# Whole modulation units through GpSimd's queue inside a recurrence

## The chip, the cores and the metric

The kernel runs on one core of one Trainium2 chip. The metric is device time in microseconds (us) of one execution, as the median of several. Engines are named as in the profile: PE is TensorE (matrix products), PEld its weight loads, DVE is VectorE, ACT is ScalarE, POOL is GpSimd and SP is SyncE. SP, ACT and POOL can each issue DMA transfers from their own instruction queue; every engine executes its queue in order.

## The reference, cut to what matters

One inference step through two layers of width 2048, for 128 context tokens and 256 latent tokens. Layer 0 runs a bidirectional RWKV-7 recurrence next to a Fourier mixer, layer 1 is windowed attention. The change concerns the modulation: each layer needs twelve blocks of 512 columns of `silu(cond) @ mod_w + mod_b`, for two conditioning vectors.

```python
def _modulation(cond, w, b):
    m = (jax.nn.silu(cond) @ w + b)[..., None, :]
    return jnp.split(m, 3, axis=-1)
...
    for layer in range(DEPTH):
        i = layer // 2
        sh_p, sc_p, g_p = _modulation(c_ctx, mod_w[layer], mod_b[layer])
        sh_s, sc_s, g_s = _modulation(c, mod_w[layer], mod_b[layer])
        hp = _rmsnorm(xp, norm_pre[layer]) * (1.0 + sc_p) + sh_p
        hs = _rmsnorm(xs, norm_pre[layer]) * (1.0 + sc_s) + sh_s
```

## The kernel before

One 512-column block of the modulation has a weight matrix of 2048 x 512 floats, 4 MB, stored as four units of 1 MB. A unit (index `u`) is 128 partitions of 2048 floats: four row blocks of 512 columns. On PE a unit takes four float32 products, each into another quarter of the rows of one PSUM tile (`ps_mod`, line 322). After the fourth unit ACT copies the sums to SBUF (`mrow`, line 327), PE folds the quarters and turns them into columns (`ps_mt`, line 331), and DVE adds the bias (line 333).

Of the 24 blocks, 8 are done at the start (`mraw`, lines 598 on), 7 inside the recurrence of layer 0 (`FILL_MODS`, the lane `fill_lane`, the tiles `rawf`), 2 on PE and 7 by sums on DVE later (`PE_MODS`, `DVE_MODS`).

The recurrence works on eight pairs of heads. Its program is written by lanes (generators), which `weave` merges by a planner's costs: each `yield pe, dve, time` says what a step costs PE and DVE and how long it lasts, and the next step comes from the lane that can start first. The lanes are the projections (`proj_cm`, products `acc`, three per weight tile: lines 398 to 400), the elementwise part (`wkv_elem`), the scores, a triangular solve (`wkv_solve`, a long run of small DVE operations, then small products `ps_z`), the chain over time (`wkv_chain`) and the norm. The fill lane puts a modulation step between them, one in every `FILL_PACE` planned microseconds. What is written first goes into an engine's queue first, with priorities shifting it a little.

Projection weights come as tiles `raw` of 256 KB through SP's queue (line 234) into two buffers; ACT splits off a rounded part `whi` (line 258), DVE the remainder `wlo` (line 259). In the recurrence the fill lane's transfers stand in the same queue of SP (line 759): each is half a unit (256 of the 512 columns of each row block, 512 KB), into two buffers. POOL does nothing but fill small tiles: `p` (line 926) and `SV` (line 1106), once per pair of heads each.

Of the kernel before, what the change touches and what calls it, by code (L numbers as in the profile page):

```python
# [11 lines left out]
F32 = mybir.dt.float32  # L12
# [15 lines left out]


FILL_MODS = [(0, 8), (0, 9), (0, 10), (0, 11), (1, 0), (1, 4), (1, 1)]  # L30
FILL_PACE = 5
PE_MODS = [(1, 5), (1, 2)]
DVE_MODS = [(1, 6), (1, 3), (1, 7)], [(1, 8), (1, 9), (1, 10), (1, 11)]

# [169 lines left out]
class Stream:  # L204
# [13 lines left out]
    def load(self):  # L218
        k = self.k
        while self.next is not None:  # L220
            x = self.next
            if x[0] == "m" and x[2] and x[2] < 4:

                self.raws.append((x, self.raw))
                self.next = next(self.it, None)
                continue
            q, n, size = (x[0],) + ((k.RAWB, 512) if x[0] == "w" else (k.MODB, 2048))
            shared = len(x) == 3 and x[2] == 0
            if self.held[q] >= n or shared and self.held["m"]:
                return  # L230
            if shared:
                self.held["m"] = k.MODB
            raw = (k.rawp if q == "w" else k.mpool).tile([128, size], F32, name="raw", tag="raw" + q, bufs=n)
            k.nc.sync.dma_start(raw, x[1])
            if q == "m":
                self.raw = raw
            self.raws.append((x, raw))
            self.held[q] += 1
            self.next = next(self.it, None)
# [64 lines left out]
class K:  # L304
# [4 lines left out]
    def mod_unit(self, raw, layer, b, u, dst, c0=0):  # L309

        nc = self.nc
        key = layer, b, c0
        n = raw.shape[1] // 4
        if u == 0:
            self.macc[key] = self.pw.tile([128, 512], F32, name="ps_mod", tag="pw")
        acc = self.macc[key]
        for i in range(4):  # L320
            kt = 4 * u + i
            nc.tensor.matmul(acc[32 * i:32 * i + 32, :n], self.silu[:, 2 * kt:2 * kt + 32], raw[:, n * i:n * i + n],  # L322
                             start=(u == 0), stop=(u == 3), skip_group_check=True)
        if u < 3:
            return
        rows = self.mpool.tile([128, n], F32, name="mrow", tag="junk", bufs=1)
        nc.scalar.copy(rows, acc[:, :n])  # L327
        ps = self.pw.tile([128, 512], F32, name="ps_mt", tag="pw")
        m0, nm = c0 // 128, n // 128
        for m in range(nm):  # L330
            nc.tensor.matmul(ps[:, 2 * m:2 * m + 2], rows[:, 128 * m:128 * m + 128], self.sel, start=True, stop=True)
        m1 = 48 * layer + 4 * b + m0
        nc.vector.tensor_tensor(dst[:, m0:m0 + nm], ps[:, 0:2 * nm].rearrange("p (m c) -> p m c", c=2),
                                self.modb[:, m1:m1 + nm].unsqueeze(2).to_broadcast([128, nm, 2]), op=ALU.add)
        del self.macc[key]
# [308 lines left out]
    def layer0_mix(self):  # L644
        tc, nc, A = self.tc, self.nc, self.A
# [25 lines left out]
        kp = self.kp = self.open("kp", "right")  # L671
# [79 lines left out]
        def fill_lane():  # L751

            self.mpool = kp
            jobs = [(layer, b, self.mod_dst(layer, b), c0, u) for layer, b in FILL_MODS for c0 in (0, 256) for u in range(4)]

            def load(layer, b, dst, c0, u):
                raw = kp.tile([128, 4, 256], F32, name="rawf", tag="rawf", bufs=2)
                w = self.mod_w(layer, b, u).rearrange("p (k c) -> p k c", k=4)
                nc.sync.dma_start(raw, w[:, :, c0:c0 + 256])
                return raw.rearrange("p k c -> p (k c)")  # L760

            raws = [load(*x) for x in jobs[:2]]
            for n, (layer, b, dst, c0, u) in enumerate(jobs):
                yield 0.5, 0, FILL_PACE
                self.mod_unit(raws.pop(0), layer, b, u, dst, c0)
                if n + 2 < len(jobs):
                    raws.append(load(*jobs[n + 2]))

        self.weave(main_lane(), chain_lane(0), chain_lane(1), norm_lane(), elem_lane((0, 2, 3, 4, 5, 6, 7)), elem_lane((1,)), proj_lane(), fill_lane(),
                   lead=LEAD)  # L770
        self.close("kp")
# [121 lines left out]
    def wkv_elem(self, j, st):  # L893

        nc, kp = self.nc, self.kp
        TT, STT, ACT = nc.vector.tensor_tensor, nc.vector.scalar_tensor_tensor, nc.scalar.activation
        SD, uni, seg = self.SD, self.uni, self.seg
        r, k, v = st["r"], st["k"], st["v"]

        yield 0.8, 0, 2.3  # L900
        up = kp.tile([128, 2, 128], F32, name="up", tag="up", bufs=1)
        nc.scalar.dma_start(up, self.A["up"][j])
        if j == 1:

            w = kp.tile([128, self.WORK], F32, name="work0", tag="work", bufs=1)
            kk, sq = w[:, 0:T], w[:, T:2 * T]
            p = w[:, 768:1548].rearrange("p (v t) -> p v t", t=65)
            tha = w[:, 1548:2316].rearrange("p (v t) -> p v t", t=64)
            E = self.TI.rearrange("p u t -> p (u t)")[:, 0:780].rearrange("p (v t) -> p v t", t=65)
        else:  # L910
            kk = kp.tile([128, T], F32, name="kk", tag="kk", bufs=1)
            sq = kp.tile([128, T], F32, name="sq", tag="tmp", bufs=1)
            p = kp.tile([128, 12, 65], F32, name="p", tag="p", bufs=1)
# [71 lines left out]
        a, b = j % 2, 2 + j % 4  # L985
# [525 lines left out]
```

## Time and profile before

| | |
|---|---|
| median of 3 runs | 1658.42 us (1656.85 to 1660.56) |
| the profiled execution | 1664.2 us |
| its span, first to last instruction | 1662.4 us |
| PE busy | 1573.7 us, 95% of the span |
| DVE busy | 1126.3 us, 68% |
| ACT busy | 774.1 us, 47% |
| POOL busy | 3.7 us |

Half units are worked on from 135.7 to 528.2 us of the span. A float32 product appears in the trace as two records, so 56 half units of four products are 448 records. A busy PE is not PE at its peak: the ends of its records are modelled, their starts are measured.

### The profile page before, as it was taken

How to read it: one execution, taken by the hardware profiler on the slowest of the kernel's cores; microseconds unless marked ns; L12 is line 12 of the kernel's file. 1: busy time of each engine (PE TensorE's matmuls, PEld its weight loads, DVE VectorE, ACT ScalarE, POOL GpSimd, SP SyncE). 2: the span in 40 equal slices, each digit the busy share in tenths (PEclk: the TensorE clock that was granted, in tenths of full speed). 3: DMA queues.
4: the chain of work that ended last, by engine and by line, in shares of the span. 5: the costliest groups of instructions: out<-in, count | busy, mean ns of one | idle time of the engine just before them, and what ended most of it. 6: DMA issues, size and time to landing. Idle time of an engine off the chain costs nothing.

```text
span 1662.4 us, 29156 instructions
## 1 busy us (share of the span) xinstructions
PE 1573.7 (95%) x11104; PEld 1304.2 (78%) x11104; DVE 1126.3 (68%) x2612; ACT 774.1 (47%) x1683; POOL 3.7 (0%) x20
## 2 busy tenths in 40 slices
PE   6789999999998998989999999899999999999998
PEld 2557777777777778879987777788888888998777
DVE  1326996797798689457664573899877999644344
ACT  3326544654745652554333333753555655333332
POOL 0000000000000000000000000000000000000000
PEclk8899997999999999999999999899999999999999
DMA  9975463253343113154456764567322334446443
GB/s 361 373 281 179 129 188 110 65 168 115 98 146 113 37 42 106 56 172 147 153 183 226 245 207 128 190 192 248 103 76 71 102 125 146 131 122 226 133 126 133
DMA packets 120243, 255.69 MB, mean 154 GB/s; under 512 B 12324, under 2 KB 45220, under 8 KB 109732
## 3 DMA queue, kind: packets, MB, share of 16 engines
q1 hardware_dynamic: 111528, 235.97, 43.6%
q10 hardware_dynamic: 8576, 17.86, 3.1%
q8 instruction: 87, 1.43, 0.4%
q14 instruction: 52, 0.43, 0.1%
HBM read 246.40 MB, written 7.39 MB: 153 GB/s over the span
## 4 chain that ended last, share of the span: by engine, by line
PE 70%; DVE 14%; DMA 7%; ACT 5%; issue 2%; SPq 0%; DVEq 0%; ACTq 0%
PE acc L398 11%; PE acc L400 11%; PE acc L399 11%; PE acct L398 5%; PE acct L399 5%; PE acct L400 5%; PE ps_mod L322 4%; DMA raw<-we 4%; DVE wlo L259 3%; DMA rawf<-modw 2%; DVE junk L345 1%; PE ps_pv L1414 1%; PE ps_v L1119 1%; PE ps_sc L1010 1%; DVE work L1039 1%
## 5 line engine op out<-in xcount | busy, mean ns | idle before, releaser
L258 ACT CAST whi<-raw 128x512 fp32r<-128x512 f32 x480 | 295.8, 620 | 479.3 <-PE acc L399 172.9
L259 DVE TENSOR_TENSOR wlo<-raw,whi 128x512 fp32r<-128x512 f32 x480 | 327.6, 688 | 262.1 <-ACT whi L258 258.8
L398 PE MATMUL acc<-hhi,whi 128*128 128x384 f32 x1376 | 480.7, 350 | 14.9 <-ACT whi L258 6.6
L400 PE MATMUL acc<-hhi,wlo 128*128 128x384 f32 x1376 | 475.3, 346 | 5.8 <-DVE wlo L259 5.6
L399 PE MATMUL acc<-hlo,whi 128*128 128x384 f32 x1376 | 475.6, 346 | 0.0
L398 PEld LDWEIGHTS acc<-hhi,whi 128*128 128x128 f32 x1376 | 263.7, 192 | 49.4 <-issue 20.2
L400 PEld LDWEIGHTS acc<-hhi,wlo 128*128 128x128 f32 x1376 | 263.8, 192 | 20.1 <-DVE wlo L259 9.5
L399 PEld LDWEIGHTS acc<-hlo,whi 128*128 128x128 f32 x1376 | 263.8, 192 | 13.0 <-issue 11.5
L345 DVE SCALAR_TENSOR_TENSOR junk<-raw,srow 128x512 f32<-128x512 f32 x224 | 154.1, 688 | 5.6 <-DMA raw<-modw 2.3
L398 PE MATMUL acct<-whi,yhi 128*128 128x512 f32 (+1 forms) x432 | 155.0, 360 | 1.2 <-DVE yb L1246 0.9
L399 PE MATMUL acct<-wlo,yhi 128*128 128x512 f32 (+1 forms) x432 | 154.7, 358 | 1.0 <-DVE wlo L259 1.0
L400 PE MATMUL acct<-whi,ylo 128*128 128x512 f32 (+1 forms) x432 | 154.3, 358 | 0.0
L398 PEld LDWEIGHTS acct<-whi,yhi 128*128 128x128 f32 x432 | 81.5, 189 | 21.8 <-DVE yb L1246 5.3
L399 PEld LDWEIGHTS acct<-wlo,yhi 128*128 128x128 f32 x432 | 81.5, 189 | 17.4 <-issue 4.2
L400 PEld LDWEIGHTS acct<-whi,ylo 128*128 128x128 f32 x432 | 81.5, 189 | 16.5 <-issue 4.4
L322 PE MATMUL ps_mod<-rawf,silu 128*32 128x256 f32 x448 | 48.8, 402 | 14.6 <-DMA rawf<-modw 14.2
L322 PE MATMUL ps_mod<-mraw,silu 128*32 128x512 f32 x256 | 35.0, 652 | 11.3 <-DMA mraw<-modw 11.3
L1047 DVE TENSOR_TENSOR work<-work 128x30 f32<-128x30 f32 (+14 forms) x120 | 39.4, 328 | 2.0
L1045 DVE TENSOR_TENSOR work<-work 128x30 f32<-128x30 f32 (+14 forms) x120 | 39.3, 328 | 1.8
L327 ACT COPY mrow<-ps_mod 128x256 f32<-128x256 f32 (+1 forms) x24 | 11.0, 460 | 60.7 <-PE ps_mod L322 60.6
L1464 DVE TENSOR_REDUCE ast<-ps_sa 128x1 f32<-128x384 f32 x64 | 25.4, 416 | 19.2 <-PE ps_sa L1455 19.1
L322 PEld LDWEIGHTS ps_mod<-rawf,silu 128*32 128x32 f32 x448 | 12.6, 110 | 32.8 <-DMA rawf<-modw 17.6
(293 smaller groups left out, 2192.8 us busy)
## 6 DMA issues: line engine op xcount, KB each, us to landing
raw<-we SPq DMA_DIRECT2D x200, 256.0 KB, 2.8
raw<-wo SPq DMA_DIRECT2D x160, 256.0 KB, 2.7
raw<-modw SPq DMA_DIRECT2D x36, 1024.0 KB, 5.0
mraw<-modw SPq DMA_DIRECT2D x32, 1024.0 KB, 9.0
rawf<-modw SPq DMA_DIRECT2D x56, 512.0 KB, 4.4
raw<-weo SPq DMA_DIRECT2D x64, 256.0 KB, 2.8
raw<-woo SPq DMA_DIRECT2D x64, 256.0 KB, 2.6
G<-gd ACTq DMA_DIRECT2D x4, 1024.0 KB, 6.9
```

What stands on the lines that cost most here:

```text
L258: k.nc.scalar.copy(hi, raw)
L259: k.nc.vector.tensor_tensor(lo, raw, hi, op=ALU.subtract)
L322: nc.tensor.matmul(acc[32 * i:32 * i + 32, :n], self.silu[:, 2 * kt:2 * kt + 32], raw[:, n * i:n * i + n], start=(u == 0), stop=(u == 3), ...
L345: nc.vector.scalar_tensor_tensor(junk, raw[:, 512 * i:512 * i + 512], 1.0, self.srow[:, c], op0=ALU.mult, op1=ALU.mult, accum_out=self.dac ...
L398: mm(out, lh, rh, start=start, stop=False)
L399: mm(out, lh, rl, start=False, stop=False)
L400: mm(out, ll, rh, start=False, stop=stop)
L1010: nc.tensor.matmul(ps[h][:, 128 * i:128 * i + 128], lh, AR[hs, :, v0 + i], start=True, stop=True)
L1039: nc.vector.transpose(X[qs], self.lane_ap(SC, q, g))
L1045: TT(tv, X[:, s + 1:32, s:s + 1].to_broadcast([128, n, s]), X[:, s:s + 1, 0:s].to_broadcast([128, n, s]), op=ALU.mult)
L1047: TT(X[:, s + 1:32, 0:s], X[:, s + 1:32, 0:s], tv, op=ALU.add)
L1464: nc.vector.tensor_reduce(st[:, 0, i:i + 1], src[i], axis=AX.X, op=ALU.max)
```

## The change

The fill lane takes whole units: 28 transfers of 1 MB in place of 56 of 512 KB, from POOL's queue in place of SP's, into one buffer in place of two of half its size. A product on such a unit has 512 columns in place of 256, so there are 112 products in place of 224. The planned pace is 10 us per unit in place of 5 us per half. The copy of the sums goes into the first columns of the unit's own buffer (`raw`) in place of a tile of its own (`mrow`), in all three places that use `mod_unit`. The small tile `up` of the elementwise part gets a second buffer.

```diff
-FILL_PACE = 5
+FILL_PACE = 10
...
-        rows = self.mpool.tile([128, n], F32, name="mrow", tag="junk", bufs=1)
+        rows = raw[:, :n]
         nc.scalar.copy(rows, acc[:, :n])
...
-            jobs = [(layer, b, self.mod_dst(layer, b), c0, u) for layer, b in FILL_MODS for c0 in (0, 256) for u in range(4)]
-
-            def load(layer, b, dst, c0, u):
-                raw = kp.tile([128, 4, 256], F32, name="rawf", tag="rawf", bufs=2)
-                w = self.mod_w(layer, b, u).rearrange("p (k c) -> p k c", k=4)
-                nc.sync.dma_start(raw, w[:, :, c0:c0 + 256])
-                return raw.rearrange("p k c -> p (k c)")
-
-            raws = [load(*x) for x in jobs[:2]]
-            for n, (layer, b, dst, c0, u) in enumerate(jobs):
-                yield 0.5, 0, FILL_PACE
-                self.mod_unit(raws.pop(0), layer, b, u, dst, c0)
-                if n + 2 < len(jobs):
-                    raws.append(load(*jobs[n + 2]))
+            jobs = [(layer, b, u, self.mod_dst(layer, b)) for layer, b in FILL_MODS for u in range(4)]
+
+            def load(layer, b, u, dst):
+                raw = kp.tile([128, 2048], F32, name="rawf", tag="rawf", bufs=1)
+                nc.gpsimd.dma_start(raw, self.mod_w(layer, b, u))
+                return raw
+
+            raw = load(*jobs[0])
+            for n, job in enumerate(jobs):
+                yield 1.0, 0, FILL_PACE
+                self.mod_unit(raw, *job)
+                if n + 1 < len(jobs):
+                    raw = load(*jobs[n + 1])
...
-        up = kp.tile([128, 2, 128], F32, name="up", tag="up", bufs=1)
+        up = kp.tile([128, 2, 128], F32, name="up", tag="up", bufs=2)
```

Lines below the fill lane move up by one in the changed kernel (926 becomes 925, 1106 becomes 1105).

First place: SP's queue where the recurrence begins. A row is a transfer, with what it waits for in brackets (the DMA marks stand for earlier transfers). Before, it reads:

```order
L759 DMA rawf<-modw 128x4x256 [waits DMAHW0_49,PE_49]
L759 DMA rawf<-modw 128x4x256
L234 DMA raw<-we 128x512 [waits DMAHW5_49,DVE_49]
L234 DMA raw<-we 128x512 [waits DMAHW6_49,DVE_49]
L759 DMA rawf<-modw 128x4x256 [waits DMAHW7_49,DMAHW0_49,PE_49]
L759 DMA rawf<-modw 128x4x256 [waits DMAHW2_49,PE_49]
L234 DMA raw<-we 128x512 [waits DMAHW4_49,DMAHW1_49,DVE_49]
L234 DMA raw<-we 128x512 [waits DMAHW6_49,DVE_49]
```

At the same place SP's queue now holds weight tiles alone:

```order
L234 DMA raw<-we 128x512 [waits DMAHW5_49,DVE_49]
L234 DMA raw<-we 128x512 [waits DMAHW6_49,DVE_49]
L234 DMA raw<-we 128x512 [waits DMAHW1_49,DVE_49]
L234 DMA raw<-we 128x512 [waits DMAHW7_49,DMAHW3_49,DVE_49]
L234 DMA raw<-we 128x512 [waits DMAHW5_49,DMAHW0_49,DVE_49]
```

No transfer of weights stands behind one of the modulation any more. Second place: POOL's queue from the start of the recurrence. Before, its first rows are:

```order
L926 MEMSET p 128x12 [waits DMAHW4_49,DMAHW2_49,DMAHW6_49,DMAHW1_49,DMAHW7_49,DMAHW0_49,PE_49]
L926 MEMSET work_1316 128x12 [waits DMAHW3_49,DMAHW5_49,DMAHW2_49,DMAHW6_49,DMAHW0_49,PE_49]
L1106 MEMSET SV 64x2x128 [waits DMAHW4_49]
L1106 MEMSET SV 64x2x128 [waits PE_49,Activation_49]
L926 MEMSET p 128x12 [waits DVE_49,Activation_49,Pool_49] x2
```

Now the transfers stand between these small fills:

```order
L758 DMA rawf<-modw 128x2048 [waits DMAHW2_49,DMAHW5_49,DMAHW1_49,DMAHW6_49,PE_49,Activation_49]
L925 MEMSET p 128x12 [waits DMAHW6_49,DMAHW4_49,DMAHW7_49,DMAHW0_49,Activation_49]
L925 MEMSET work_1294 128x12 [waits DMAHW3_49,DMAHW5_49,DMAHW0_49,DMAHW6_49,PE_49,Activation_49]
L1105 MEMSET SV 64x2x128 [waits DMAHW4_49]
L1105 MEMSET SV 64x2x128
L758 DMA rawf<-modw 128x2048 [waits DMASW0_49,PE_49]
L758 DMA rawf<-modw 128x2048 [waits DMASW1_49,PE_49]
L758 DMA rawf<-modw 128x2048 [waits DMASW2_49,PE_49]
L925 MEMSET p 128x12 [waits DVE_49,Activation_49,Pool_49]
L758 DMA rawf<-modw 128x2048 [waits DMASW3_49,PE_49,Activation_49]
```

Each transfer waits for PE, that is for the four products on the unit before it (and every fourth also for ACT's copy and the products that read it), because there is one buffer. Third place: PE's queue in the chain of the third pair of heads, where a row is a product with its count. Before:

```order
L322 MATMUL ps_mod<-rawf,silu 32x256 x5
L1158 MATMUL ps_o<-AR,work_3781 64x64 x8
L1165 MATMUL ps_s<-work_3781,BT 64x64 x8
L1119 MATMUL ps_v<-cmat,v 64x128
L1119 MATMUL ps_v<-cmat,work_3781 64x128
L1138 MATMUL ps_p_4200<-SV,SC 64x64 x4
L1178 MATMUL ps_o<-SC,work_3781 64x64 x8
L322 MATMUL ps_mod<-rawf,silu 32x256 x3
L400 MATMUL acc<-hhi,wlo 128x384
L1010 MATMUL ps_sc<-AR,BK 128x128 x2
L1146 MATMUL ps_y<-work_3781,TI 64x64 x4
L322 MATMUL ps_mod<-rawf,silu 32x256 x4
```

In the change, somewhat later in the same chain:

```order
L322 MATMUL ps_mod<-rawf,silu 32x512 x4
L1009 MATMUL ps_sc<-AR,BK 128x128 x8
L1019 MATMUL ps_bt<-cmat,BK 128x128
L1137 MATMUL ps_p_4293<-SV,SC 64x64 x4
L1019 MATMUL ps_bt<-cmat,BK 128x128 x5
L1205 MATMUL ps_m<-o,cmat 128x384
L1019 MATMUL ps_bt<-cmat,BK 128x128
L1145 MATMUL ps_y<-work_3637,TI 64x64 x4
L1019 MATMUL ps_bt<-cmat,BK 128x128 x3
L1009 MATMUL ps_sc<-AR,BK 128x128 x5
L322 MATMUL ps_mod<-rawf,silu 32x512 x4
```

A whole unit now stands where half units stood, and between two units PE has the products of the nine rows in the middle: during these the next 1 MB has to be asked for, moved and landed.

## Rows read from the trace of the kernel before

**Rows 1.** The page: its head.

```profile
span 1662.4 us, 29156 instructions
```

**Rows 2.** Tile `rawf`: PE's records, first and last start; transfers from issue to landing.

```profile
L322 PE MATMUL ps_mod<-rawf,silu x448: 376/379/637, 135.7 to 528.2; 128*32 128x256 f32 x150
...
DMA to landing us min/median/max: 3.7/4.4/7.8
```

**Rows 3.** Waits of PE, 130 to 530 us: total, times, longest.

```profile
PE ps_mod L322 <- DMA rawf<-modw: 14.2, 13, 4.2
PE ps_z L1063 <- DVE work L1053: 3.2, 3, 1.2
```

**Rows 4.** Waits of SP's queue and of ACT, 130 to 530 us.

```profile
SPq L759 <- PE ps_mod L322: 98.4, 33, 17.0
...
ACT whi L258 <- DMA raw<-we: 39.1, 25, 4.6
```

**Rows 5.** Busy us by stage: length, PE, PEld, DVE, ACT, POOL; clock, DMA share, GB/s.

```profile
480.00:530.00 50.00, 44.14 (x300) 35.82 (x292) 44.31 (x116) 24.27 (x46) 0.00 (x0) 0.97 0.55 171
...
250.00:260.00 10.00, 8.99 (x125) 7.17 (x125) 9.89 (x11) 3.57 (x7) 0.00 (x0) 0.92 0.46 155
260.00:270.00 10.00, 10.00 (x59) 8.98 (x59) 6.59 (x9) 1.55 (x3) 0.12 (x1) 0.50 0.01 2
390.00:400.00 10.00, 7.84 (x127) 6.58 (x126) 9.89 (x8) 2.93 (x6) 0.00 (x0) 0.91 0.51 156
520.00:530.00 10.00, 8.37 (x74) 6.77 (x74) 9.97 (x16) 4.42 (x11) 0.00 (x0) 0.83 0.40 127
```

**Rows 6.** PE in order of time: start, length; half units between projection products.

```profile
350.72 0.33 PE L400 MATMUL acc<-hhi,wlo 128*128 128x384 f32 x1
350.89 0.34 PE L398 MATMUL acc<-hhi,whi 128*128 128x384 f32 x1
351.16 0.62 PE L322 MATMUL ps_mod<-rawf,silu 128*32 128x256 f32 x2
351.71 0.45 PE L399 MATMUL acc<-hlo,whi 128*128 128x384 f32 x1
352.09 0.62 PE L322 MATMUL ps_mod<-rawf,silu 128*32 128x256 f32 x2
...
364.97 1.07 PE L322 MATMUL ps_mod<-rawf,silu 128*32 128x256 f32 x16
365.97 0.44 PE L398 MATMUL acc<-hhi,whi 128*128 128x384 f32 x1
```

**Rows 7.** The same view later: products of 512 columns on whole units.

```profile
830.21 1.05 PE L322 MATMUL ps_mod<-raw,silu 128*32 128x512 f32 x2
831.18 0.44 PE L398 MATMUL acc<-hhi,whi 128*128 128x384 f32 x1
831.55 1.04 PE L322 MATMUL ps_mod<-raw,silu 128*32 128x512 f32 x2
```

**Rows 8.** The page's DMA issues: count, size of one, median us to landing.

```profile
raw<-modw SPq DMA_DIRECT2D x36, 1024.0 KB, 5.0
mraw<-modw SPq DMA_DIRECT2D x32, 1024.0 KB, 9.0
```

**Rows 9.** PE in order of time in the chain: what the small products take.

```profile
457.59 1.16 PE L1010 MATMUL ps_sc<-AR,BK 64*128 64x128 f32 x16
458.68 0.77 PE L1020 MATMUL ps_bt<-cmat,BK 128*128 128x128 f32 x5
459.38 0.45 PE L1138 MATMUL ps_p<-SV,SC 128*64 128x64 f32 x8
...
460.10 0.83 PE L1206 MATMUL ps_m<-o,cmat 128*128 128x384 f32 x2
```

**Rows 10.** PE's longest wait for a half unit, at 521.63 us.

```profile
521.63 1.08 PE L322 MATMUL ps_mod<-rawf,silu 128*32 128x256 f32 x8 [4.24 <-DMA rawf<-modw]
```

**Rows 11.** DVE's largest copy between SBUF tiles, 130 to 530 us: count, busy, mean ns.

```profile
L1078 DVE COPY TI<-SC 64x768 f32<-64x768 f32 x8 | 4.4, 552 | 0.2
```

## The prediction

> **What bounds the kernel now.** I read first where the changed tile lives. The half units are worked on from 135.7 to 528.2 us [rows 2], so some 392 of the span's 1662.4 us [rows 1] are in question; what is done before and after is the same work. Next, who is waited for there. PE waits 14.2 us in that stretch for half units, and the next cause is 3.2 us [rows 3]: PE's own queue is the bound, and the modulation is both part of its work and the largest cause of its pauses. The busy times by stage qualify that. Toward the end of each triangular solve DVE is full: 9.89 of 10 us in two of them, 9.97 in the third [rows 5]. The small products that open the next step wait for DVE there, so PE's time in a solve is partly free. Last, SP's queue: for 98.4 us it stands before a half unit's transfer until PE has freed the buffer, with projection weights queued behind, and ACT waits 39.1 us for such weights [rows 4]. PE hardly feels this: no wait for a weight tile reaches even the 3.2 us of the second cause [rows 3].
>
> **The change part by part.**
>
> *PE's work on the units.* A product of 256 columns alone between two projection products costs 352.09 - 351.16 = 0.93 us for the pair; a projection product alone steps by 350.89 - 350.72 = 0.17 us, so the half-unit product costs 0.76. Up to four together run side by side on quarters of the array and I charge the same 0.76. Eight together take 365.97 - 364.97 = 1.00 us, with entry and exit 1.1 [rows 6]. In PE's order before I count 62 groups of up to five products and 7 of eight: 62 x 0.76 + 7 x 1.1 = 54.8 us. A group of 512 columns costs 831.55 - 830.21 - 0.17 = 1.17 us [rows 7]; the changed order has 41 groups of up to four: 48.0 us. **Gain 6.8 us**: twice the columns cost only one and a half times as much.
>
> *The waits for the units.* With one buffer, a unit's transfer is asked for when PE has finished the unit before it, and has to land before PE reaches the next. Between two units PE has other work, which I summed from its order. In the place shown in the section on the change it is 8 + 5 score products (458.68 - 457.59 = 1.09 us for eight), ten transposes (5 records in 0.70 us, two records each: 2.8), and the small rest (0.4 + 0.7 + 0.3): 5.9 us [rows 9]. Elsewhere it is mostly about 30 projection products, 5.3 us. The 27 gaps run from 3.8 to 19.6 us; 9 are at most 5.3, 16 at most 7.0. Summed this way, PE's work from the first half unit to the last is 356 us, against 392 in the trace [rows 2], 14.2 of which are the waits; so I stretch each gap by (392 - 14)/356 = 1.06.
>
> The latency to compare, from PE's last product to the landed megabyte, is the disputed number: nothing in the trace is issued by POOL. The nearest row is a transfer of the same bytes in the same layout by SP, 5.0 us (36 of them); the worst is 9.0, at the start, where transfers crowd [rows 8]. Even the half units took 3.7 to 7.8 [rows 2]. I take 6.3: the 5.0, plus somewhat over 1 us of my own choosing for the hop from PE to POOL, for making the transfer there and for weights in flight. The shortfalls sum to 3.8 us at a latency of 5.5, 8.4 at 6.0, 11.9 at 6.3, 21.6 at 7.0, 29.3 at 7.5 and 37.9 at 8.0. The slope is what matters: near 7 us, half a microsecond of latency costs 7.
>
> *What DVE hides.* Of the 14.2 us that go, the largest wait, 4.24 us [rows 10], stands where DVE is full [rows 5], and I count it as worth nothing: 10.0 us gained. Of the 11.9 that come, about 2.2 belong to gaps inside the first two solves: 9.7 lost. **Net gain 0.3 us.**
>
> *Where the units stand.* The changed order ends its units earlier, after 1028 projection products of the stretch instead of 1182. The last four half units, 4 x 0.76 = 3.0 us of PE, stood in the third solve, where DVE has 44.31 of 50 us [rows 5]; now they are in the chain before it, where PE has no slack. **Loss 3.0 us.**
>
> *SP's queue.* Half units leave it, and their 98.4 us of standing no longer hold weights back. PE's benefit is bounded by nothing below and by some 4 us above (the small waits of which the 3.2 is the largest). **Gain 2 us.** The weights still share the transfer engines with the same bytes.
>
> *POOL's queue.* The fills of `p` and `SV` stand among the transfers and can hold one back. I followed each in the order: what a fill waits for (a product or a DVE step of the pair before) lies before the unit that the next transfer waits for. Nothing. Conversely, a fill behind a transfer waits at most for PE's previous unit, long before its tile is used.
>
> *Small edits.* The copy in the unit's buffer keeps one buffer in four until the folding products have read it, about 2 us more. At the start there are seven buffers; three transfers start 1 to 2 us later by the order. **Loss 1 us.** The second `up` buffer: its one buffer is not among PE's waits, nothing.
>
> The sum is -6.8 - 0.3 + 3.0 - 2.0 + 1.0 = -5.1 us, on the profiled execution 1664.2 to 1659. The median of the runs lies 5.8 us below that execution, so I predict 1653.
>
> A page speaks about the disputed number. The Trainium skill, "DMA: Bandwidth & Descriptors", section "Measured (HBM→SBUF, 128 partitions, SWDGE, issued from GpSimd)", gives 6.15 us for 1 MB of GpSimd's transfers, without the making of descriptors. With a further 0.9 us for that, the latency would be near 7.0 and the sum about +2 us instead of -5; no run here shows it yet.
>
> **The rivals.**
>
> *POOL's transfers are slow (slower).* At a latency of 7.5 us the waits cost 29.3 - 7.4 hidden = 21.9 against 10.0, and the sum becomes +7; at 8.0, 28.0 against 10.0, and +13. It decides from about 6.9 us on. For it: the half units already needed up to 7.8 us [rows 2]. Against: 5.0 us for the same bytes with weights alongside [rows 8]. One mechanism that would do this is a transfer that cannot be made while DVE holds something that POOL needs. The candidates in this stretch are DVE's copies between SBUF tiles; the largest kind is 8 copies of 0.55 us, 4.4 us together [rows 11], so it would touch few of the 28 transfers, and by about half a microsecond. If every DVE instruction counted, DVE being busy nearly nine tenths of the time, each transfer would come about 1 us later, latency 7.3, +4 us. The Trainium skill, "SBUF — State Buffer", section "SBUF: two separate sides", warns of this for copies in DVE's fast mode and says to issue from ACT or SP instead.
>
> *POOL's transfers are quick and SP's relief counts (clearly faster).* At 5.5 us the waits cost 3.6 and the sum is -6.8 - 6.4 + 3 - 2 + 1 = -11; with 4 us from SP's queue, -13, a median of 1645. For it: the 5.0 us. Against: that latency has not yet a hop to another queue.
>
> *The change does not touch the bound (no change).* If the solves set the pace by DVE and the chains by their own latency, PE's savings and waits both vanish: within 3 us of 1658. For it: DVE's 9.9 of 10 [rows 5]. Against: the 14.2 us, of which only 4.2 lie there.
>
> One thing I can't price: PE's clock is at half speed in some spots after a solve (0.50 of 2.4 GHz, which is 1.2 GHz, from 260 to 270 us, after a stretch in which PE paused and moved to small products [rows 5]). Another pattern of pauses may lengthen or shorten such a spot by 5 us or so; it widens the range.
>
> **How the numbers follow.** Latency 5.8 to 6.7, the forecast (-8 to -1 us): 0.40. Below that: 0.17. No effect: 0.13. Above, or clock spots added: 0.30. A measurement can tell about 0.2%, 3.3 us, from no change. Of the forecast about three quarters is beyond that, so faster is 0.30 + 0.17 = 0.47, same 0.10 + 0.11 = 0.21, slower 0.32 with a little of the "no effect" case. The range reaches from the quick case with a clock spot less, 1638, to a latency of 8.3 us, 1678. The forecast's own range is 1648 to 1658.
>
> **What would show it.** Right: records of `rawf` products fall from 448 to 224; their waits on PE total 8 to 16 us, spread over about 12 units, mostly those with 30 projection products between; landing times of 5 to 6 us; ACT's wait for `we` weights clearly under 39; SP's waits at the fill lane gone. Wrong: landing times of 7 us or more with waits above 20, or POOL's fills waited for by the chain, or waits below 5 us and still no gain, which would mean that DVE or the chain sets the pace.

## The result and the profile after

| | before | changed |
|---|---|---|
| median | 1657.63 us (1656.02 to 1660.56, 4 runs) | 1674.06 us (1669.51 to 1680.23, 4 runs) |
| the profiled execution, its span | 1664.2, 1662.4 us | 1680.23, 1678.4 us |
| mean granted clock of that execution (1.00 is 2.4 GHz) | 0.972 | 0.960 |

The change makes the kernel slower: ratio 1.0100, 95% interval 1.0060 to 1.0139, some 16 us. The forecast was 1653, with 1638 to 1678. That 1674 lies inside this range is luck: its upper end was put there for slow transfers, which did not come.

Differences between kernels below are taken from their ratios to the kernel before, times 1658 us, because each group of kernels ran beside its own runs of the kernel before.

The rows that answer to [rows 2]: tile `rawf` of the changed kernel, with its durations as min/median/max in ns, first and last start in us, and the landing times of its transfers.

```profile
L322 PE MATMUL ps_mod<-rawf,silu x224: 592/617/1063, 135.2 to 502.9; 128*32 128x512 f32 x112
...
L758 POOL DMA_DIRECT2D rawf<-modw x28: 527/527/662, 112.4 to 496.8; - x28
...
DMA to landing us min/median/max: 5.0/5.2/8.0
```

And to [rows 3] and [rows 4], for the changed kernel from 130 to 530 us: the waits of PE, SP's queue, ACT and DVE (total us, times, longest).

```profile
PE ps_mod L322 <- DMA rawf<-modw: 8.7, 8, 3.3
...
SPq L234 <- DVE wlo L259: 209.9, 36, 37.7
...
ACT whi L258 <- DMA raw<-we: 40.9, 19, 4.9
...
DVE wlo L259 <- ACT whi L258: 31.4, 21, 5.7
```

Two of these rows have no counterpart in [rows 4]. In the kernel before they are:

```profile
SPq L234 <- DVE wlo L259: 97.3, 35, 12.3
...
DVE wlo L259 <- ACT whi L258: 16.7, 17, 2.4
```

Read the first row against [rows 3]: the waits for units fell from 14.2 to 8.7 us, further than to the 11.9 that were forecast. The disputed transfer is quick, 5.2 us in the median, with a few stragglers up to 8.0. And still 16 us are lost, so the loss isn't where the prediction spent most of its working.

It shows first in the granted clock. The view of busy times by stage gives it (length, busy us and records of PE, PEld, DVE, ACT and POOL, then clock, DMA share and GB/s). This is the recurrence of the kernel before:

```profile
130.00:740.00 610.00, 574.03 (x5442) 465.29 (x5442) 467.42 (x1046) 323.87 (x682) 2.75 (x12) 0.96 0.38 115
```

And of the changed kernel: the recurrence, and 30 us around the end of its third triangular solve.

```profile
130.00:740.00 610.00, 569.59 (x5086) 454.96 (x5085) 455.68 (x1012) 313.83 (x659) 17.02 (x39) 0.92 0.33 104
...
540.00:550.00 10.00, 6.30 (x52) 5.92 (x53) 9.97 (x22) 4.59 (x10) 0.00 (x0) 0.85 0.18 52
550.00:560.00 10.00, 10.00 (x137) 8.36 (x136) 8.33 (x8) 1.73 (x3) 0.00 (x0) 0.50 0.15 46
560.00:570.00 10.00, 10.00 (x57) 6.75 (x55) 2.50 (x6) 3.10 (x9) 0.00 (x0) 0.50 0.04 11
```

A clock of 0.92 in place of 0.96 over 610 us is 98 us at half speed in place of 49. Work that runs at half speed takes about twice as long (a product below takes 1.76 us in place of 0.97), so each us of it loses about half a us: by this estimate 24 us more are lost. The pattern is that of [rows 5]: DVE is full (9.97 of 10) at the solve's end, PE pauses (6.30), and then it gets only 1.2 GHz for the next 20 us, where it looks fully busy. At the same place the kernel before does better:

```profile
515.00:525.00 10.00, 5.76 (x30) 4.63 (x29) 9.90 (x28) 5.97 (x14) 0.00 (x0) 0.83 0.61 198
525.00:535.00 10.00, 10.00 (x158) 8.76 (x157) 9.89 (x7) 4.09 (x8) 0.00 (x0) 1.00 0.12 28
535.00:545.00 10.00, 10.00 (x106) 7.07 (x103) 3.67 (x9) 3.30 (x9) 0.00 (x0) 0.83 0.18 56
545.00:555.00 10.00, 9.46 (x107) 8.22 (x106) 7.79 (x20) 8.18 (x16) 0.38 (x1) 0.83 0.00 0
```

PE pauses there too, and for longer (5.76 busy of 10), yet the next 10 us run at full clock. So a pause at the solve's end does not settle by itself what clock follows.

What the lower level costs a single product is seen in PE's order of time in the changed kernel, at one place of full and one of half speed.

```profile
341.11 1.04 PE L322 MATMUL ps_mod<-rawf,silu 128*32 128x512 f32 x2
342.08 0.33 PE L1019 MATMUL ps_bt<-cmat,BK 128*128 128x128 f32 x1
...
432.67 1.83 PE L322 MATMUL ps_mod<-rawf,silu 128*32 128x512 f32 x2
434.43 0.44 PE L400 MATMUL acc<-hhi,wlo 128*128 128x384 f32 x1
```

The step is 342.08 - 341.11 = 0.97 us in one, 434.43 - 432.67 = 1.76 us in the other. Six of the changed kernel's 41 groups were met at half speed.

Part of the loss comes back later. DVE's scaling of the output rows marks the end of layer 0; before and changed:

```profile
L1287 DVE TENSOR_SCALAR xr<-yb,rs x3: 1280/1281/1286, 1048.0 to 1056.6; 128x2048 f32<-128x2048 f32 x3
```

```profile
L1286 DVE TENSOR_SCALAR xr<-yb,rs x3: 1281/1283/1286, 1062.3 to 1071.0; 128x2048 f32<-128x2048 f32 x3
```

The last product of the recurrence's chain starts at 719.0 before and 741.8 after (+22.8), this row at +14.3. So some 8 us are regained between the two, in a stretch that the prediction left out.

### The profile page after: what moved, and what is told of

Same layout as the page of the kernel before. It is cut to its first block, busy times and chain, and to the rows that moved or that the text cites. A ratio compares the mean times of both kernels' runs of the same rounds, so it can differ in the third digit from the quotient of the medians.

```text
span 1678.4 us, 28665 instructions
## 1 busy us (share of the span) xinstructions
PE 1581.9 (94%) x10880; PEld 1311.0 (78%) x10880; DVE 1125.2 (67%) x2605; ACT 773.7 (46%) x1676; POOL 18.6 (1%) x48
## 4 chain that ended last, share of the span: by engine, by line
PE 69%; DVE 14%; DMA 9%; ACT 4%; issue 3%; DVEq 0%; ACTq 0%; SPq 0%; POOL 0%; POOLq 0%
PE acc L398 10%; PE acc L400 10%; PE acc L399 10%; PE acct L398 5%; PE acct L399 5%; PE acct L400 5%; PE ps_mod L322 4%; DMA raw<-we 3%; DVE wlo L259 3%; DMA rawf<-modw 3%; DMA mraw<-modw 2%; PE ps_v L1118 1%; PE ps_pv L1413 1%; PE ps_z L1069 1%; PE ps_s L1164 1%
## 5 line engine op out<-in xcount | busy, mean ns | idle before, releaser
L400 PEld LDWEIGHTS acc<-hhi,wlo 128*128 128x128 f32 x1376 | 264.8, 193 | 28.1 <-DVE wlo L259 14.5
L398 PEld LDWEIGHTS acct<-whi,yhi 128*128 128x128 f32 x432 | 81.8, 190 | 18.9 <-DVE yb L1245 4.8
L322 PE MATMUL ps_mod<-rawf,silu 128*32 128x512 f32 x224 | 47.9, 652 | 8.9 <-DMA rawf<-modw 8.7
L1463 DVE TENSOR_REDUCE ast<-ps_sa 128x1 f32<-128x384 f32 x64 | 25.4, 415 | 19.4 <-PE ps_sa L1454 19.1
L1009 PEld LDWEIGHTS ps_sc<-AR,BK 64*128 64x128 f32 x384 | 27.7, 187 | 12.3 <-issue 6.0
L1011 DVE TENSOR_TENSOR SC<-ps_sc,cmat 128x512 f32<-128x512 f32 x48 | 31.0, 682 | 8.3 <-PE ps_sc L1009 8.1
```

The source lines that it names most:

```text
L398: mm(out, lh, rh, start=start, stop=False)
L400: mm(out, ll, rh, start=False, stop=stop)
L1009: nc.tensor.matmul(ps[h][:, 128 * i:128 * i + 128], lh, AR[hs, :, v0 + i], start=True, stop=True)
L1011: nc.vector.tensor_tensor(SC[:, 12 * h + v0:12 * h + v0 + 4, :], ps[h].rearrange("p (a t) -> p a t", a=4), self.mask.unsqueeze(1).to_broad ...
L1463: nc.vector.tensor_reduce(st[:, 0, i:i + 1], src[i], axis=AX.X, op=ALU.max)
```

## The experiments

Sixteen kernels. With each stand its median, the ratio to the kernel before with its interval, and the half-speed time: twice (1 - mean clock) times the run's time, as a mean over its runs. The kernel before has 74 to 81 us of it. Letters for theories in the expectations hold within their own group: e1 to e4, e5 to e8, f1 to f4, g1 to g4.

| kernel | units | queue | median, us | ratio (95%) | half-speed, us |
|---|---|---|---|---|---|
| changed | whole | POOL | 1674.06 | 1.0100 (1.0060 to 1.0139) | 126 |
| e1_after_sp | whole | SP | 1665.42 | 1.0047 (1.0028 to 1.0066) | 124 |
| e4_pace12 | whole | POOL | 1676.83 | 1.0116 (1.0070 to 1.0163) | 140 |
| f3_whole_lead | whole | SP | 1676.74 | 1.0107 (1.0068 to 1.0146) | 126 |
| g1_whole_pool_lead | whole | POOL | 1678.72 | 1.0114 (1.0083 to 1.0145) | 136 |
| g2_whole_sp_pace12 | whole | SP | 1657.94 | 1.0000 (0.9978 to 1.0022) | 113 |
| f2_pairs | two halves in one step | SP | 1666.74 | 1.0054 (1.0025 to 1.0082) | 120 |
| f1_two_steps | whole, in two steps | SP | 1665.99 | 1.0053 (1.0024 to 1.0082) | 100 |
| e2_half_pool | half | POOL | 1671.95 | 1.0066 (1.0042 to 1.0090) | 90 |
| e3_rows | half | SP | 1649.92 | 0.9951 (0.9931 to 0.9972) | 89 |
| f4_rows_lead | half | SP | 1650.11 | 0.9966 (0.9947 to 0.9985) | 87 |
| g3_rows_pool | half | POOL | 1666.33 | 1.0056 (1.0031 to 1.0080) | 101 |
| g4_rows_pool_lead | half | POOL | 1669.36 | 1.0061 (1.0031 to 1.0091) | 103 |
| e5_sp_pace | half | SP | 1676.74 | 1.0117 (1.0094 to 1.0139) | 93 |
| e6_pool_pace | half | POOL | 1677.07 | 1.0124 (1.0103 to 1.0145) | 97 |
| e7_sp_lead | half | SP | 1660.66 | 1.0021 (0.9998 to 1.0044) | 79 |
| e8_pool_lead | half | POOL | 1677.09 | 1.0121 (1.0096 to 1.0145) | 100 |

### The parts of the change one by one

**e1_after_sp**: the changed kernel with SP's queue.

```diff
-                nc.gpsimd.dma_start(raw, self.mod_w(layer, b, u))
+                nc.sync.dma_start(raw, self.mod_w(layer, b, u))
```

> The changed kernel with its 28 whole units through SP's queue again, one buffer, all else as changed. The theory that the loss lies in whole units standing elsewhere in PE's order, with PE's clock at half speed for 95 us of the recurrence in place of 51, expects no cure: 1668 to 1680 us, recurrence some 20 us longer than before. The rival, that transfers from POOL's queue (its small fills among them, or DVE in their way) cost the time, expects 1650 to 1660.

Measured: 8.8 us below the changed kernel, still 7.8 above the kernel before, so between the two expectations. The half-speed time stays at 124 us: the low clock came with the units, not with the queue. But the queue does show in PE's waits. Through SP a unit lands 4.9 us after the start of its issue in the median, through POOL 5.2, and from 130 to 530 us PE waits 4.0 us for units in e1, 8.7 in the changed kernel:

```profile
PE ps_mod L322 <- DMA rawf<-modw: 4.0, 5, 1.4
...
DMA to landing us min/median/max: 4.8/4.9/6.1
```

So 4.7 of the 8.8 us may be longer waits for the units themselves; the two kernels differ in their orders as well.

**e2_half_pool**: the kernel before with POOL's queue, and nothing else.

```diff
-                nc.sync.dma_start(raw, w[:, :, c0:c0 + 256])
+                nc.gpsimd.dma_start(raw, w[:, :, c0:c0 + 256])
```

> The kernel before with its 56 half units through POOL's queue in place of SP's, two buffers, nothing else. The theory of order and clock expects 1653 to 1661 us: PE's waits for half units 10 to 18 us, half-speed time in the recurrence 45 to 65 us. The rival, that POOL's queue costs the time, expects 1668 or more.

Measured: +10.9 us, as the rival expected, with PE's waits for half units down to 6.2 us and a half-speed time of 90 us against 81. So the queue's cost is not PE's wait for the transfer here, and the clock takes only some 4 us of it. The rest is met again below.

**e3_rows**: the kernel before with the copy in the unit's buffer, and nothing else.

```diff
-        rows = self.mpool.tile([128, n], F32, name="mrow", tag="junk", bufs=1)
+        rows = raw[:, :n]
```

> The kernel before with the copy of the sums in the unit's own buffer, nothing else. If the 8 us that the changed kernel wins back in the output projection of layer 0 come from this edit (18 groups of modulation products there in place of 27, at 1.17 us each), it gives 1647 to 1652 us, with the recurrence unchanged within 3 us. If they come from the later arrival of the changed kernel at that stage, it gives 1655 to 1660.

Measured: -8.1 us, faster than both kernels, as the first expectation had it. In its trace the row of DVE above is met 15 us earlier than in the profile of the kernel before, whose profiled execution lies 5.8 us above its median:

```profile
L1287 DVE TENSOR_SCALAR xr<-yb,rs x3: 1281/1281/1286, 1032.7 to 1041.4; 128x2048 f32<-128x2048 f32 x3
```

In PE's order the other blocks (`raw`, after the recurrence) form 18 groups of products instead of 27, 11 of them single products instead of 23. Nine groups at 831.18 - 830.21 = 0.97 us [rows 7] are 8.7 us. The changed kernel has the same 18. From the last product of the chain to that row of DVE pass 329.0 us before (719.0 to 1048.0), 321.4 in e3 (711.3 to 1032.7) and 320.5 in the changed kernel, so the gain does arise in this stretch. In the kernel before, `mrow` shares its one buffer (the tag `junk`) with the products of DVE's sums there. That the regrouping is the whole reason is an inference from this agreement.

**e4_pace12**: the changed kernel with a slower plan, to put the last units where the half units stood.

```diff
-FILL_PACE = 10
+FILL_PACE = 12
```

> The changed kernel with a planned pace of 12 us per unit in place of 10, so that the last unit stands after 1212 projection products (1028 in the change, 1200 before) and three units stand in the third solve again. If the place of the units makes the loss, 1650 to 1662 us and a half-speed time in the recurrence under 70 us. If it is whole units or POOL's transfers as such, 1668 to 1680.

Measured: 2.7 us above the changed kernel, within the error, with 140 us at half speed. Its last unit stands behind 1212 projection products instead of 1028, as far on as the half units before, so units that end too early are not the reason for the low clock. But the plan also left 67 projection products behind the recurrence (1601 of them stand before the chain's last product, 1668 without the edit), so the pace tells two things at once.

### Is it the order alone?

Each edit gives another order of hundreds of rows on PE, also where the edit only names a queue. Two edits that add or remove no work test what that is worth, each with either queue: the pace 5.2 in place of 5, and the priority of the fill lane.

```diff
-FILL_PACE = 5
+FILL_PACE = 5.2
...
-LEAD = (0, 300, 300, 0, 0, 0, 0, 100)
+LEAD = (0, 300, 300, 0, 0, 0, 0, 110)
```

> The kernel before with the planned pace of its half units at 5.2 in place of 5: the same work and the same queues in another order. Theory A (an order of instructions is worth little; POOL's queue itself costs some 10 us): within 4 us of the kernel before. Theory B (the order that the scheduler happens to make is worth some 10 us by itself, and the loss with POOL's queue was such an order): this kernel and the one with the lead changed differ from the kernel before by 5 us or more, either way.

> The kernel before with its half units through POOL's queue, at the planned pace of 5.2. Theory A: 9 to 13 us above the same edit through SP's queue, as at the pace of 5 (12.6). Theory B: no fixed sign; within 5 us of the same edit through SP's queue, or below it.

> The kernel before with the lead (priority) of the fill lane 110 in place of 100: the same work in a slightly other order. Theory A: within 4 us of the kernel before. Theory B: off by 5 us or more, either way.

> The kernel before with half units through POOL's queue and the lead 110. Theory A: 9 to 13 us above the same lead through SP's queue. Theory B: no fixed sign; within 5 us of it, or below it.

Measured against the kernel before: pace alone +19.4 us, lead alone +3.5 us (from 0 to +7). With POOL's queue on top: +1.2 with the pace, +16.6 with the lead. The result is mixed. The pace turned out to be no pure test of the order: it too leaves 67 projection products behind the recurrence (1601 against 1668). The lead shows what an order is worth by itself, a few us. Whole units with that lead (f3, below) stand 9.9 us above e1, half units with the copy in the buffer (f4) 2.5 above e3. One pair can therefore not price POOL's queue.

### What lowers the clock

**f1_two_steps**: e1 with each whole unit worked on in two steps of 256 columns, other work between.

```diff
...
-                yield 1.0, 0, FILL_PACE
-                self.mod_unit(raw, *job)
+                layer, b, u, dst = job
+                yield 0.5, 0, FILL_PACE / 2
+                self.mod_half(raw, layer, b, u, 0)
+                yield 0.5, 0, FILL_PACE / 2
+                self.mod_half(raw, layer, b, u, 1)
+                if u == 3:
+                    self.mod_unit(raw, *job, done=True)
```

The new function `mod_half` makes the four products on one range of 256 columns, and the two ranges share one PSUM tile. The values of the modulation do not come out as the reference's, so this kernel stands for the time alone; the products are those described.

> The changed kernel with SP's queue, whole units loaded, but worked on in two steps of 256 columns with other work between. Theory A (PE's clock falls because a unit's products are twice as wide and stand twice as far apart): mean granted clock back from 0.963 to 0.972 or more, time 1645 to 1656. Theory C (it falls because of what came with the units, the one buffer, the transfers or the copy into it): clock 0.960 to 0.966, time 1662 to 1670.

**f2_pairs**: e3 with two half units in one step. Transfers, buffers, queue and products are those of e3.

```diff
-                yield 0.5, 0, FILL_PACE
+                if n % 2 == 0:
+                    yield 1.0, 0, 2 * FILL_PACE
                 self.mod_unit(raws.pop(0), layer, b, u, dst, c0)
```

> The kernel before with the copy in the unit's buffer, half units loaded by SP into two buffers, but worked on two at a time, one step in 10 planned us: products of 256 columns, eight together. Theory A: the clock falls as with whole units, 0.960 to 0.967, time 1658 to 1672. Theory C: clock 0.971 to 0.976, time 1645 to 1655.

**f3_whole_lead** and **f4_rows_lead**: e1 and e3 with the lead 110 (the edit shown above).

> The changed kernel with SP's queue and the lead 110 in place of 100: whole units in another order. If the low clock belongs to whole units (A or C): 0.959 to 0.967 again, time 1660 to 1673. Theory B (the low clock was an accident of one order): 0.970 or more, time 1645 to 1657.

> The kernel before with the copy in the unit's buffer and the lead 110. If the 8 us won by that copy are its own: 6 to 12 us below the kernel before with the lead 110 (which ran 1660.7), 1648 to 1655. Theory B (they were an accident of one order): 1656 to 1664.

Measured: f2 is the case nearest to a single edit. Against e3 it loses (1.0054 - 0.9951) x 1658 = 17.1 us; its half-speed time is 120.0 - 88.5 = 31.5 us longer, which costs half of that, 15.8. So most of the loss is the clock, without one wide product and without POOL. A second part must not be passed over: PE also stands idle longer. Here are e3, f2 and, for comparison, e1 from 130 us to the start of the chain's last product:

```profile
130.00:711.30 581.30, 548.88 (x5343) 444.32 (x5342) 457.06 (x1023) 315.29 (x668) 2.75 (x12) 0.96 0.36 111
```

```profile
130.00:729.60 599.60, 557.57 (x5350) 454.05 (x5349) 458.94 (x1025) 315.63 (x669) 2.50 (x12) 0.94 0.35 108
```

```profile
130.00:722.60 592.60, 557.97 (x5121) 449.65 (x5119) 457.75 (x1016) 316.19 (x661) 2.76 (x12) 0.94 0.34 109
```

Length less PE's busy time is 32.4 us in e3 and 42.0 in f2, 9.6 more; the closer grouping gives back 5.6 (its groups sum to 41.0 us, those of e3 to 46.6). More idle time in all is not what lowers the clock, though: e1, with whole units, is idle 34.6 us, little more than e3, and has 124 us at half speed against 89.

f3 repeats the low clock in another order (126 us; its time lies above the expectation), f4 the gain of the copy (-5.6 us; the expectation's comparison with e7 gives 10.6 in medians). f1, which spaces the work again, falls from 124 to 100 us (mean clock 0.970, between the two expectations), where e3 has 89. Its time didn't follow: multiplied by the clock, which takes the half-speed part out, it is 1616 us against 1604 in e1, so this order gave away elsewhere what the clock returned, and f1 alone would not carry the point. Over all 17 kernels the rule holds without exception: a unit or two halves in one step, 113 to 140 us at half speed; spaced in halves, at most 103.

### What POOL's queue costs

Four more kernels complete four pairs that differ in the queue alone: the changed kernel with the lead 110, e4 with SP's queue, and e3 and f4 with POOL's. Their edits are those shown.

> The changed kernel with the lead 110: whole units through POOL's queue. Its partner with SP's queue (whole units, lead 110) ran 1676.7. If POOL's queue has a price of its own of 8 to 13 us: 1684 to 1692. If it has none and the earlier differences came from the order: 1668 to 1682. In both the mean clock stays at 0.958 to 0.967, as with every kernel that works a whole unit in one step.

> The changed kernel with the planned pace 12 and SP's queue. Its partner with POOL's queue ran 1676.8. If POOL's queue has a price of its own: 1663 to 1669. If it has none: 1670 to 1682. Clock 0.956 to 0.967.

> The kernel before with the copy in the unit's buffer, its half units through POOL's queue. Its partner with SP's queue ran 1649.9. Price of its own: 1658 to 1663. None: 1644 to 1655. Clock 0.969 to 0.977, as with every kernel that spaces its half units.

> The same with the lead 110. Its partner with SP's queue ran 1650.1. Price of its own: 1658 to 1663. None: 1644 to 1655. Clock 0.969 to 0.977.

| pair: with POOL's queue, with SP's | POOL less SP, us | half of the longer half-speed time, us | PE longer idle to the chain's end, us | DVE's waits for `whi`, 130 to 560 us: SP, POOL |
|---|---|---|---|---|
| e2, before | +10.9 | +4.2 | +6.1 | 16.7, 26.9 |
| e6, e5 | +1.2 | +2.0 | +2.3 | 20.8, 25.2 |
| e8, e7 | +16.6 | +10.4 | +3.0 | 18.9, 23.7 |
| changed, e1 | +8.8 | +1.0 | +5.8 | 12.2, 32.8 |
| g1, f3 | +1.2 | +4.8 | -1.4 | 18.6, 26.9 |
| e4, g2 | +19.2 | +13.4 | +9.5 | 13.1, 21.1 |
| g3, e3 | +17.4 | +6.2 | +10.2 | 14.5, 25.7 |
| g4, f4 | +15.8 | +8.4 | +10.3 | 18.5, 23.4 |

POOL's queue is slower in all eight, by 11.4 us in the mean (95% interval 5.4 to 17.4, from the spread of the eight), though the two of +1.2 are within the noise. It has a price of its own; its size hangs on the order. Single expectations were missed on both sides: g1 falls where no price was expected, g2 ran below both of its ranges, and g3 and g4 lie above theirs.

The third and fourth columns show where the price stands on PE. The third comes from the mean clock of all runs, the fourth from the profiled executions: length less busy time, from 130 us to the start of the chain's last product. In the mean the clock takes 6.3 us and idle time 5.7, and in each pair the two add up to the price within 4 us. This is an account and not yet a cause. The row of g3, against that of e3 above (42.6 us idle, 32.4 there):

```profile
130.00:731.10 601.10, 558.48 (x5352) 451.11 (x5354) 458.20 (x1027) 315.85 (x671) 42.85 (x66) 0.95 0.34 106
```

The last column is a symptom that all eight share: DVE waits longer for the rounded part of the projection weights. e3 (SP) from 130 to 530 us:

```profile
DVE wlo L259 <- ACT whi L258: 14.0, 15, 2.8
...
PE ps_mod L322 <- DMA rawf<-modw: 11.5, 12, 2.8
```

g3 (POOL), the same stretch:

```profile
DVE wlo L259 <- ACT whi L258: 25.7, 22, 3.9
...
PE ps_mod L322 <- DMA rawf<-modw: 9.4, 10, 1.9
```

In the five pairs with half units PE's waits for units get shorter with POOL's queue while the elementwise engines wait longer; in the three with whole units they get longer (3.1 to 8.6 us in g1 against f3). DVE is full at the ends of the solves [rows 5], so a wait there delays what PE needs next. That this is the path by which PE's idle time and the low clock arise is argued, not shown: the queue also changes the order of hundreds of DVE's operations, and no run held that order fixed.

## Why the prediction was wrong

The time moved the other way from the forecast. The forecast's sum was -5.1 us; the parts as measured are -8.1 for the copy in the buffer (e3), (1.0047 - 0.9951) x 1658 = +15.9 for whole units and the second `up` buffer (e1 against e3), and +8.8 for POOL's queue (the changed kernel against e1): +16.6, which is the result (each part is one step from the kernel before over e3 and e1 to the changed kernel, so they must add up).

- **The clock is the step that failed.** The prediction saw the half-speed spots [rows 5], said that it couldn't price them, and put "5 us or so" into the range only; in the sum the clock stands at nothing. The half-speed time grew by some 47 us, from about 79 to 126, which costs about 23. For the step from e3 to e1 it is (124 - 89)/2 = some 18 us, more than the +15.9 of that step. The prediction took whole units for the same work at a lower price; with them PE's filler work became half as many pieces twice as far apart. f2 shows such a loss with columns, transfers and queue as in e3.
- **PE's work on units: right, then taken away by the clock.** Forecast -6.8. In e1 the groups, each from its start to the start of the next other product, sum to 37.2 us against 45.9 before, -8.7. In the changed kernel, with six groups at half speed, they sum to 45.0.
- **Waits for units: mechanism right, size better than forecast.** 8.7 us over 8 waits, where 11.9 over some 12 were forecast from a latency of 6.3. By the prediction's own table, 8.4 us belong to a latency of 6.0. That small differences of latency count was right too: with SP's 4.9 us in place of 5.2, e1 has 4.0 us of waits. The slow-transfer rival, which carried most of the chance of a loss, was wrong: landing is 5.2 us.
- **Place of the units, +3: not isolated.** In the trace the last half unit stands after 1200 projection products, where the prediction counted 1182. The pace moves projection products as well. With SP's queue the slower pace won 7.8 us (g2 against e1), with POOL's it won nothing (e4).
- **SP's queue, -2: wrong sign.** One exchange of queues measures this term and the next together: -2 was forecast for the two, +8.8 came. ACT's wait for weights was to fall clearly under 39; it is 40.9, and DVE's wait behind it rose from 16.7 to 31.4. Freed of the half units, SP stands before the weights' own two buffers instead: 209.9 us, where it was 97.3, until `wlo` is made and the buffer is free.
- **POOL's queue, "nothing": wrong by 9 us here, 11 in the mean.** The fills were followed rightly: neither in the changed kernel nor in e2 or e8 does another engine wait for a fill of POOL. What was left out shows on PE as lower clock and longer idle time: in the mean of the pairs about equal parts, in the changed kernel against e1 1.0 and 5.8 us. That it comes from weights which the half units no longer hold back, so that every weight is split at another time, is argued.
- **Small edits, +1: wrong sign.** The copy alone is -8.1, half of one per cent of the time in one line. The order showed the nine missing groups beforehand; the prediction looked at the fill lane's groups only.

On the two pages that were cited. The Trainium skill, "DMA: Bandwidth & Descriptors", section "Measured (HBM→SBUF, 128 partitions, SWDGE, issued from GpSimd)", gives 6.15 us for 1 MB, without the making of descriptors; here the median is 5.2 us from the start of POOL's issue to landing, with the making in it, and the measurement decides. The Trainium skill, "SBUF — State Buffer", section "SBUF: two separate sides", warns of transfers that can't be made while DVE copies in its fast mode. No sign of it here: the 28 issues on POOL took 527 ns in the median and 662 at most. With only a few such copies in the stretch [rows 11] this is no strong test.

## What to carry to other kernels

Filler work that keeps TensorE going between pauses is worth more than its own time: halve the number of its pieces and the clock may take back twice what the pieces save (here some 18 us, from e3 to e1, against 8.7), so count the half-speed time (one minus the granted clock, by stage) ahead of the waits. Where a scheduler sets the order, read the groups of products that an edit makes everywhere in the program, not only at the edit, and price a queue from several orders: a single pair here would have said anything from 1 to 19 us. And a queue that stands before a full buffer may be doing useful pacing; the time it stands is no gain until somebody is shown to wait for it.

## What was not expected of the hardware

At the same work, queue and transfers, two groups of four small products in one step instead of in two moved the mean granted clock over the kernel from 0.973 to 0.964 (e3, f2). POOL's own issue of a transfer took 527 ns for whole units and 748 ns for half units, almost without spread, although the half units carry half the bytes (each partition's in four pieces):

```profile
L759 POOL DMA_DIRECT2D rawf<-modw x56: 748/748/882, 112.0 to 518.1; - x56
```

This row is from e8; its counterpart stands among the changed kernel's rows in the section on the result. Why one step instead of two lowers the clock, and which of the pauses it is, stays open; so does the path by which POOL's queue brings PE idle time and a lower clock.
